# A decoder layer on one core: first x tile on another queue and engine, attention's small products grouped and pinned, the recurrence's diagonal with level 0

## Chip, cores, metric

One core of a Trainium2 chip runs the kernel. The metric is the device time of one execution in microseconds. Engines are named as in the profile: PE (TensorE), PEld (its weight loads), DVE (VectorE), ACT (ScalarE), POOL (GpSimd) and SP (SyncE, which issues most transfers).

## What is computed

One layer on 256 tokens with 2048 features, all in float32:

```
h = RMSNorm(x)
[q_a|k_a|v_a|q_r|f_r|i_r|g_r|gate_a|gate_r] = h @ w_in
A: causal attention, 8 heads of 128, q and k normed per head, partly rotated
R: HGRN2: f = lb + (1-lb) sigmoid(f_r), k = 1-f, q = silu(q_r)
   S_t = diag(f_t) S_{t-1} + k_t i_t^T,  o_t = S_t^T q_t
   o_r = RMSNorm per head (o) * sigmoid(g_r)
y = sigmoid(gate_a + b_a) * (o_a @ w_up_a) + sigmoid(gate_r + b_r) * (o_r @ w_up_r)
x = x + y @ w_out
x = x + relu(RMSNorm(x) @ w_mlp1)^2 @ w_mlp2
```

With 256 tokens there is a single attention block, so the choice of past blocks falls away and attention is plain causal attention.

## The kernel before

Every weight matrix is read in units of 128 x 2048 numbers (1 MB). A unit is loaded by SP into `raw`, ScalarE rounds it to `hi` (float32r), and VectorE makes the rest `lo = raw - hi`. Activations are cut in the same two parts, side by side in tiles called `xcat`, `oac`, `orc` and so on. A product of two matrices is then three streamed products, hi x hi, lo x hi and hi x lo, with 512 columns each, or one of 512 and one of 256 columns where the weights are the stationary side. `cut(u)` (line 170) makes the halves of unit u; `unit()` (line 196) hands out a unit and cuts the one two places ahead. `raw`, `hi` and `lo` have three buffers each. In the stages that stream the weights (`by_tokens`, line 695, and the first loop, line 341) a unit is 24 products, and its second product already wants `lo`.

The units come in this order: 16 for v and i (`pv`), 40 for the projections to q, k, f, g in feature-major form (`project`, groups of two units, `pw`), then for each half of the output columns 16 units of gates (`pg`) and 8 units of the two up-projections (`pr` for the recurrence's output, `pa` for attention's), then w_out and the MLP. TensorE takes the stream's products one after the other; eleven products on zeros (`WARM`, line 231) stand in front.

Beside the stream run generators: `prepare` (line 291, row norms of x, biases, the lower bound lb), `attend` (599), `enter` and `recur` (421, 444) and `recur_out` (572). `step()` (line 207) advances the first two of the list `side` after each group of stream products, by as much work as their yields declare against a budget of 2.8 or 3.6 us. Where one of their small products is issued, it lands in TensorE's order between the stream's: an insertion. The final order on each engine is settled when the program is built, by a scheduler that follows dependencies and its own estimates; `tc.issue_after(x)` keeps an instruction from standing ahead of x.

`attend` makes, for a group of four heads, the scores (`pl`) of the first 128 queries, their softmax, the transposes (`ptr`), then the same for the second 128, then the products with v (`po`). `recur` makes the diagonal blocks of the recurrence (`pd`, line 456), then eight levels, each of which needs q and k multiplied on by the level before. `recur_out` norms the output (`head_rms`, line 550: `pb`, logarithm, exponential on ScalarE), gates it and cuts it into `orc`. `drain()` (line 218) runs all generators to their end ahead of the up-projections.

At the start SP issues the first unit in four pieces with x's tiles in between (`load`, line 146; `load_x`), ScalarE's queue issues the vectors `vt`, and `parts_of_x` (271) cuts x, scaled by the norm's gain, into `xcat`: the high part on ScalarE, the rest on VectorE.

Of the kernel before, what the change touches and what calls it, by code (L numbers as in the profile page):

```python
# [9 lines left out]
F32 = mybir.dt.float32  # L10
# [16 lines left out]
WARM = 11  # L27
# [3 lines left out]
def layer_kernel(ctx: ExitStack, tc: tile.TileContext, xT, vecs, wv, wm, wg, wu, wo, w1, w2, cf, cm, out):  # L31
# [106 lines left out]

    raws = {}
# [6 lines left out]
    def load(u):  # L146
# [3 lines left out]
        for s in pieces(u):  # L150
            if u < 4:
                load_x(u, s)
# [17 lines left out]
    def cut(u):  # L170
# [9 lines left out]
        split[u] = (hi, lo)  # L180
        if u in beside:
# [45 lines left out]
    nc.scalar.dma_start(vt, vecs)  # L227
    warm = pool["g"].tile([P, 512], F32R, tag="g", name="warm")
    nc.vector.memset(warm.bitcast(F32), 0.0)
# [30 lines left out]
    nc.vector.memset(ones_r.bitcast(F32), 1.0)  # L260
    ones = cp.tile([P, P], F32, name="ones")
    nc.vector.memset(ones, 1.0)
    eps_t = cp.tile([P, 1], F32, name="eps_t")
    nc.vector.memset(eps_t, EPS)
    lsc_t = cp.tile([P, 1], F32, name="lsc_t")
    nc.vector.memset(lsc_t, float(-0.5 * np.log(128.0)))
# [22 lines left out]
    lb = cp.tile([P, 2, NH], F32, name="lb")  # L289

    def prepare():
# [28 lines left out]
        lbm = cp.tile([P, NH], F32, name="lbm")  # L320
        lbe = cp.tile([P, 2, NH], F32, name="lbe")
        nc.vector.tensor_max(lbm, lbl[:, 0, :], lbl[:, 1, :])
        for i in range(2):
            nc.vector.tensor_sub(lbe[:, i, :], lbl[:, i, :], lbm)
        nc.scalar.activation(lbe, lbe, AF.Exp)
        nc.vector.tensor_add(lbm, lbe[:, 0, :], lbe[:, 1, :])
        nc.vector.reciprocal(lbm, lbm)
        nc.vector.tensor_mul(lb[:, 0, :], lbe[:, 0, :], lbm)
        nc.vector.tensor_scalar(lb[:, 1, :], lb[:, 0, :], -1.0, 1.0, op0=OP.mult, op1=OP.add)
# [11 lines left out]
    for c in range(4):  # L341
        pst = [bank(f"pv{t}", pm) for t in range(2)]
        for q in range(4):
            hi, lo = unit()
            hi, lo = (x.rearrange("p (k f) -> p k f", k=4) for x in (hi, lo))
            for k in range(4):
                kk = 4 * q + k
                for t in range(2):
                    xh = xcat[:, kk, t * P : (t + 1) * P]
                    xl = xcat[:, kk, T + t * P : T + (t + 1) * P]  # L350
                    nc.tensor.matmul(pst[t], xh, hi[:, k, :], start=(kk == 0), stop=False)  # L351
                    nc.tensor.matmul(pst[t], xh, lo[:, k, :], start=False, stop=False)  # L352
                    nc.tensor.matmul(pst[t], xl, hi[:, k, :], start=False, stop=(kk == KD - 1))  # L353
# [850 lines left out]
```

## Time and profile before

| | |
|---|---|
| time, median of 3 runs | 1388.30 us (1388.20 to 1388.41) |
| the profiled execution: its time, its span | 1388.16 us, 1386.4 us |
| mean granted TensorE clock | 0.999 |
| PE busy | 1380.2 us (100%) |
| PEld, DVE, ACT, POOL busy | 1180.4, 1085.4, 793.6, 82.4 us |
| HBM | 260 GB/s over the span |

The span runs from the first to the last instruction; 1.8 us of the execution lie around it. Busy time of PE is the union of its products with modelled ends, so 100% does not say that each product ran at its best. In the rows further below, times are microseconds from the span's start.

### The profile page before, as it was taken

The numbers are of one execution on the slowest core, as the hardware profiler recorded it, in microseconds if no ns is written. First come the engines' busy times: TensorE is split into PE (matmuls) and PEld (weight loads), VectorE is DVE, ScalarE is ACT, GpSimd is POOL, SyncE is SP. The second block draws the span as 40 slices with busy tenths as digits, with TensorE's granted clock in tenths as the row PEclk, the third lists the DMA queues.
The fourth block names the chain that finished last, engine by engine and source line by source line (L and its number), as shares of the span: only waits on it lengthen the run. The fifth ranks groups of instructions, "written<-read, shape, count | busy, mean of one in ns | idle before, by whom it ended". The sixth has DMA issues, their size and how long they took to land.

```text
span 1386.4 us, 19141 instructions
## 1 busy us (share of the span) xinstructions
PE 1380.2 (100%) x7886; PEld 1180.4 (85%) x7886; DVE 1085.4 (78%) x971; ACT 793.6 (57%) x747; POOL 82.4 (6%) x132
## 2 busy tenths in 40 slices
PE   9999999999999999999999999999999999999998
PEld 7888888888888888888888888888888888888887
DVE  7656789877957776678755979989898888989875
ACT  7444566764457443434445677666666666656652
POOL 0111101001000111111100000000000000000000
PEclk9999999999999999999999999999999999999999
DMA  8898877566765999898966686777868777686772
GB/s 304 312 349 316 304 276 249 202 218 199 258 215 172 333 329 318 294 333 295 324 225 223 223 295 220 260 256 256 288 213 277 239 271 242 241 306 228 278 230 87
DMA packets 108153, 362.35 MB, mean 261 GB/s; under 512 B 8176, under 2 KB 10496, under 8 KB 87840
## 3 DMA queue, kind: packets, MB, share of 16 engines
q1 hardware_dynamic: 88880, 294.99, 61.4%
q0 software_dynamic: 17888, 65.04, 13.0%
q8 instruction: 62, 1.02, 0.3%
q10 hardware_dynamic: 1296, 1.09, 0.3%
q14 instruction: 27, 0.22, 0.0%
HBM read 327.52 MB, written 33.57 MB: 260 GB/s over the span
## 4 chain that ended last, share of the span: by engine, by line
PE 98%; DVE 0%; DMA 0%; ACT 0%; issue 0%; SPq 0%; DVEq 0%
PE pw L368 21%; PE pw L370 11%; PE pw L378 11%; PE pw L381 5%; PE pg L691 4%; PE pg L693 4%; PE pg L692 4%; PE ps L691 3%; PE ps L692 3%; PE ps L693 3%; PE py L691 2%; PE py L692 2%; PE py L693 2%; PE pv L352 2%; PE pv L353 2%; PE pv L351 2%
## 5 line engine op out<-in xcount | busy, mean ns | idle before, releaser
L179 DVE TENSOR_TENSOR lo<-raw,hi 128x2048 fp32r<-128x2048 f32 (+2 forms) x130 | 275.4, 2124 | 133.4 <-ACT hi L178 120.8
L178 ACT ACTIVATE hi<-raw 128x2048 fp32r<-128x2048 f32 (+2 forms) x130 | 231.1, 1782 | 237.4 <-PE pg L693 56.5
L788 DVE TENSOR_TENSOR low<-w,hiw 128x2048 fp32r<-128x2048 f32 x135 | 308.7, 2286 | 66.2 <-ACT hiw L787 63.2
L787 ACT ACTIVATE hiw<-w 128x2048 fp32r<-128x2048 f32 x135 | 258.5, 1915 | 149.3 <-PE pw L368 63.1
L368 PE MATMUL pw<-x2cat,hiw 128*128 128x512 f32 x1024 | 242.8, 389 | 0.0
L368 PEld LDWEIGHTS pw<-x2cat,hiw 128*128 128x128 f32 x1024 | 191.6, 188 | 39.5
L378 PE MATMUL pw<-xcat,hi 128*128 128x512 f32 x640 | 150.2, 391 | 0.0
L378 PEld LDWEIGHTS pw<-xcat,hi 128*128 128x128 f32 x640 | 119.2, 188 | 24.5
L370 PEld LDWEIGHTS pw<-x2cat,low 128*128 128x128 f32 x1024 | 131.3, 191 | 5.0
L370 PE MATMUL pw<-x2cat,low 128*128 128x256 f32 x1024 | 132.8, 283 | 0.0
L691 PE MATMUL pg<-hi,xcat 128*128 128x512 f32 x256 | 100.7, 393 | 0.0
L693 PE MATMUL pg<-hi,xcat 128*128 128x512 f32 x256 | 99.7, 389 | 0.0
L692 PE MATMUL pg<-lo,xcat 128*128 128x512 f32 x256 | 99.7, 389 | 0.0
L788 DVE TENSOR_TENSOR low<-b,hiw 128x2048 fp32r<-128x2048 f32 x35 | 80.2, 2290 | 21.0 <-ACT hiw L787 20.9
L787 ACT ACTIVATE hiw<-b 128x2048 fp32r<-128x2048 f32 x35 | 67.0, 1915 | 30.5 <-PE ps L693 20.3
L381 PEld LDWEIGHTS pw<-xcat,lo 128*128 128x128 f32 x640 | 79.4, 192 | 1.6
L381 PE MATMUL pw<-xcat,lo 128*128 128x256 f32 x640 | 79.9, 283 | 0.0
L368 PE MATMUL pw<-mcat,hi 128*128 128x512 f32 x256 | 61.8, 392 | 0.0
L693 PEld LDWEIGHTS pg<-hi,xcat 128*128 128x128 f32 x256 | 48.1, 188 | 10.1
L691 PEld LDWEIGHTS pg<-hi,xcat 128*128 128x128 f32 x256 | 48.1, 188 | 9.9
L692 PEld LDWEIGHTS pg<-lo,xcat 128*128 128x128 f32 x256 | 48.1, 188 | 9.7
L368 PEld LDWEIGHTS pw<-mcat,hi 128*128 128x128 f32 x256 | 46.9, 188 | 9.0
(266 smaller groups left out, 2234.6 us busy)
## 6 DMA issues: line engine op xcount, KB each, us to landing
w<-w SPq DMA_DIRECT2D x107, 1024.0 KB, 5.6
raw<-wm SPq DMA_DIRECT2D x56, 1024.0 KB, 7.1
wt<-w POOLq DMA_DIRECT2D x56, 512.0 KB, 7.7
t<-wt POOLq DMA_DIRECT2D x56, 512.0 KB, 7.1
w<-t SPq DMA_DIRECT2D x28, 1024.0 KB, 5.1
b<-w SPq DMA_DIRECT2D x21, 1024.0 KB, 6.3
raw<-wg SPq DMA_DIRECT2D x16, 1024.0 KB, 7.1
raw<-wu SPq DMA_DIRECT2D x16, 1024.0 KB, 7.7
```

Source lines behind the costliest of these rows:

```text
L178: nc.scalar.activation(hi[:, s], raw[:, s], AF.Copy)
L179: low = nc.vector.tensor_sub(lo[:, s], raw[:, s], hi[:, s].bitcast(F32))
L351: nc.tensor.matmul(pst[t], xh, hi[:, k, :], start=(kk == 0), stop=False)
L368: nc.tensor.matmul(pst, h, cat, start=(first and i == 0), stop=False)
L370: nc.tensor.matmul(pst[:, T:], l, cat[:, :T], start=False, stop=(last and i == n - 1))
L378: nc.tensor.matmul(pst, h, cat, start=(i == 0), stop=False)
L381: nc.tensor.matmul(pst[:, T:], l, cat[:, :T], start=False, stop=(i == len(parts) - 1))
L691: nc.tensor.matmul(pst, xh, hi[:, k], start=(begin and k == 0), stop=False)
L692: nc.tensor.matmul(pst, xh, lo[:, k], start=False, stop=False)
L693: nc.tensor.matmul(pst, xl, hi[:, k], start=False, stop=(end and k == 3))
L787: nc.scalar.activation(hi, r, AF.Copy)
L788: newest[0] = nc.vector.tensor_sub(lo, r, hi.bitcast(F32))
```

## The change

- The four tiles of x that go with the first unit are loaded by four issues of ScalarE's queue, right behind `vt`, in tiles of 128 x 256. SP's list starts with the four pieces of the first unit.
- The high part of x's first tile is made by VectorE (`tensor_scalar`), the other fifteen by ScalarE as before. In the first unit the three products of the two token halves are issued as hi, hi, lo-of-x, lo-of-x, lo, lo.
- Ten warm-up products in place of eleven. Four small memsets come behind the one that clears the warm-up tile. The lower bound lb is computed after the low half of unit 8.
- `attend` makes the scores of both query halves in one insertion, then one reciprocal and both multiplications, then all transposes, then all products with v. Transposes and value products may not stand ahead of the newest product of the stream in `ws_group`.
- `recur` issues the diagonal and level 0 without a yield in between; the diagonal's products may not stand ahead of `rqp`.
- The up-projection of attention's output comes first, the recurrence's second, and the units of `wu` are loaded in that order.

```diff
-WARM = 11
+WARM = 10
...
-        units += [block(wu, c, at) for c in two for at in (2, 3, 0, 1)]
+        units += [block(wu, c, at) for c in two for at in range(4)]
...
         for s in pieces(u):
-            if u < 4:
+            if 0 < u < 4:
                 load_x(u, s)
...
+    xr.append(g4("xr", (P, 4, T)))
+    for k in range(4):
+        nc.scalar.dma_start(xr[0][:, k, :], xT[0][:, k, :])
     warm = pool["g"].tile([P, 512], F32R, tag="g", name="warm")
...
-            nc.scalar.activation(xcat[:, k, :T], src, AF.Copy, scale=g_in[:, k : k + 1])
+            if k == 0:
+                nc.vector.tensor_scalar(xcat[:, k, :T], src, g_in[:, :1], 1.0, op0=OP.mult, op1=OP.mult)
+            else:
+                nc.scalar.activation(xcat[:, k, :T], src, AF.Copy, scale=g_in[:, k : k + 1])
...
+        with tc.issue_after(lows[8].ins):
+            lower_bound()
...
+                products = [[(p, xh, hi, 0), (p, xh, lo, 1), (p, xl, hi, 2)] for p, xh, xl in tokens]
+                if c + q == 0:
+                    products = [[a[i] for a in products] for i in (0, 2, 1)]
...
+                with tc.issue_after(entered[-1].ins):
+                    nc.tensor.matmul(
+                        pd[32 * b : 32 * b + 32, i * 32 : (i + 1) * 32],
+                        kss[g][:, h, c], qs[g][:, h, c], start=True, stop=True,
+                    )
...
-        yield 0.7
         for lv in range(LEVELS):
...
-            yield 1.5 * (t + 1)
-            nc.vector.reciprocal(sm[:, c], sm[:, c])
-            nc.vector.tensor_mul(l, l, sm[:, c][:, :, None].to_broadcast([P, 4, w]))
-            yield 0.6 * (t + 1) + 0.2
+        yield 4.0
+        nc.vector.reciprocal(sm, sm)
+        for t, l in both:
+            c = slice(4 * t, 4 * t + 4)
+            nc.vector.tensor_mul(l, l, sm[:, c][:, :, None].to_broadcast([P, 4, (t + 1) * P]))
+        yield 5.6
+        for t, l in both:
             for s in range(t + 1):
                 ptr = bank("ptr")
-                for h in range(4):
-                    nc.tensor.transpose(ptr[:, h * P : (h + 1) * P], l[:, h, s * P : (s + 1) * P], ident)
+                with tc.issue_after(stream_end[0].ins):
+                    for h in range(4):
+                        nc.tensor.transpose(ptr[:, h * P : (h + 1) * P], l[:, h, s * P : (s + 1) * P], ident)
...
-            yield 0.1
+        yield 5.6
         for b in range(2):
             po = bank("po")
...
-            for pst in by_tokens(orc, "pr"):
+            for pst in by_tokens(oac, "pa"):
                 pass
...
-            for q, pst in enumerate(by_tokens(oac, "pa")):
+            for q, pst in enumerate(by_tokens(orc, "pr")):
```

The built program's order shows where this leaves the instructions. ScalarE, from the recurrence's last norm to the first units of the up-projections, before (`sq_3843` is the second head group's factor, `orc_3972` and `orc_3975` are the first group's output, `hi_3982` is the first unit of `pr`):

```order
L565 ACT_TABLE_LOAD
L565 ACTIVATE sq_3843<-pb_3931,eps_t 128x512
L565 ACTIVATE sq_3843<-pb_3935,eps_t 128x512
L178 ACTIVATE hi_3942<-raw_3940 128x2048
L568 ACT_TABLE_LOAD
L568 ACTIVATE sq_3843<-sq_3843 128x1024
L410 ACTIVATE orc_3972<-ro_3773 128x2x256
L410 ACTIVATE orc_3975<-ro_3773 128x2x256
L178 ACTIVATE hi_3982<-raw_3980 128x2048
```

The same stretch in the change, from the wider start of the norm on (`hi_3992` is the second unit of `pa`, `hi_4056` the first of `pr`):

```order
L180 ACTIVATE hi_3992<-raw_3990 128x2048
L589 ACT_TABLE_LOAD
L589 ACTIVATE sq_3907<-pb_3977,eps_t 128x512
L589 ACTIVATE sq_3907<-pb_3981,eps_t 128x512
L592 ACT_TABLE_LOAD
L592 ACTIVATE sq_3907<-sq_3907 128x1024
...
L747 ACT_TABLE_LOAD
L747 ACTIVATE gate_4033<-gate_4033 128x512
L592 ACT_TABLE_LOAD
L592 ACTIVATE sq_3945<-sq_3945 128x1024
L432 ACTIVATE orc_4038<-ro_3873 128x2x256
L432 ACTIVATE orc_4041<-ro_3873 128x2x256
L180 ACTIVATE hi_4056<-raw_4054 128x2048
```

Both norms' factors, with a gate's sigmoid between, now stand in one run behind `hi_3992`, and the next unit's hi comes only after them.

VectorE in that stretch, before:

```order
L411 TENSOR_TENSOR orc_3972<-ro_3773,orc_3972 128x2x256
L411 TENSOR_TENSOR orc_3975<-ro_3773,orc_3975 128x2x256
L577 SCALAR_TENSOR_TENSOR ro_3790<-ro_3790,vt,sq_3843 128x1024
L179 TENSOR_TENSOR lo_3983<-raw_3980,hi_3982 128x2048
L578 TENSOR_TENSOR ro_3790<-ro_3790,sgr_2730 128x1024
L179 TENSOR_TENSOR lo_4019<-raw_4016,hi_4018 128x2048
```

and in the change:

```order
L602 TENSOR_TENSOR ro_3873<-ro_3873,sgr_2456 128x1024
L601 SCALAR_TENSOR_TENSOR ro_3890<-ro_3890,vt,sq_3945 128x1024
L433 TENSOR_TENSOR orc_4038<-ro_3873,orc_4038 128x2x256
L433 TENSOR_TENSOR orc_4041<-ro_3873,orc_4041 128x2x256
L602 TENSOR_TENSOR ro_3890<-ro_3890,sgr_2678 128x1024
L181 TENSOR_TENSOR lo_4057<-raw_4054,hi_4056 128x2048
L433 TENSOR_TENSOR orc_4046<-ro_3890,orc_4046 128x2x256
```

`lo_4057`, the low half of `pr`'s first unit, moved behind the scaling, the cutting and the gating of the recurrence's output.

TensorE where `pr` begins in the change (`pa` ends above it, with the third of its products):

```order
L724 MATMUL pa_306_4053<-hi_3992,oac_2901 128x512
L722 MATMUL pr_307_4118<-hi_4056,orc_4038 128x512
L722 MATMUL pr_308_4119<-hi_4056,orc_4038 128x512
L723 MATMUL pr_307_4118<-lo_4057,orc_4038 128x512
L724 MATMUL pr_307_4118<-hi_4056,orc_4038 128x512
```

and before:

```order
L693 MATMUL pg_297_3898<-hi_3942,xcat 128x512
L691 MATMUL pr_305_4053<-hi_3982,orc_3972 128x512
L692 MATMUL pr_305_4053<-lo_3983,orc_3972 128x512
L693 MATMUL pr_305_4053<-hi_3982,orc_3972 128x512
L691 MATMUL pr_305_4053<-hi_3982,orc_3972 128x512
```

In the change 48 products lie between the last `pb` and `pr`, before 72; and the first two products of `pr` are now both of the hi half.

## Rows read from the trace of the kernel before

**Rows 1.** The page, part 4: the chain that ended last, by engine.

```profile
PE 98%; DVE 0%; DMA 0%; ACT 0%; issue 0%; SPq 0%; DVEq 0%
```

**Rows 2.** Timeline, TensorE, start: start us, us, line, tile, count [idle <-releaser].

```profile
1.46 4.76 PE L232 MATMUL pwarm<-warm 128*128 128x512 f32 x11 [1.46 <-DVE warm L229]
...
6.37 0.19 PEld L351 LDWEIGHTS pv<-hi,xcat 128*128 128x128 f32 x1 [0.57 <-ACT xcat L274]
...
10.04 0.39 PE L351 MATMUL pv<-hi,xcat 128*128 128x512 f32 x1
```

**Rows 3.** Timeline, TensorE, 420 to 428 us: the two last norms' products.

```profile
420.41 0.39 PE L563 MATMUL pb<-sqh,ones_r 128*128 128x512 f32 x1
...
421.33 0.39 PE L691 MATMUL pg<-hi,xcat 128*128 128x512 f32 x1
...
426.78 0.39 PE L563 MATMUL pb<-sqh,ones_r 128*128 128x512 f32 x1
...
427.71 0.39 PE L691 MATMUL pg<-hi,xcat 128*128 128x512 f32 x1
```

**Rows 4.** Timeline, TensorE: value products of both groups; the stream behind an insertion.

```profile
259.08 0.39 PE L653 MATMUL po<-pt,v 128*128 128x128 f32 x2
...
261.68 1.63 PE L378 MATMUL pw<-xcat,hi 128*128 128x512 f32 x6
...
310.22 0.39 PE L653 MATMUL po<-pt,v 128*128 128x128 f32 x2
...
313.11 7.54 PE L378 MATMUL pw<-xcat,hi 128*128 128x512 f32 x32
...
342.54 0.50 PE L691 MATMUL pg<-hi,xcat 128*128 128x512 f32 x1
342.87 0.39 PE L692 MATMUL pg<-lo,xcat 128*128 128x512 f32 x1
```

**Rows 5.** Timeline, ScalarE, 420 to 440 us: norm of the recurrence's output.

```profile
420.61 1.92 ACT L178 ACTIVATE hi<-raw 128x2048 fp32r<-128x2048 f32 x1 [3.53 <-PE pg L693]
422.54 1.28 ACT L565 ACT_TABLE_LOAD   x1
423.84 1.27 ACT L565 ACTIVATE sq<-pb,eps_t 128x512 f32<-128x512 f32 x2
...
426.42 0.63 ACT L716 ACTIVATE gate<-gate 128x512 f32<-128x512 f32 x1
...
428.36 1.06 ACT L568 ACTIVATE sq<-sq 128x1024 f32<-128x1024 f32 x1
...
438.04 1.14 ACT L410 ACTIVATE orc<-ro 128x512 fp32r<-128x512 f32 x2
```

**Rows 6.** Timeline, VectorE, 439 to 447 us.

```profile
439.13 1.28 DVE L411 TENSOR_TENSOR orc<-ro,orc 128x512 fp32r<-128x512 f32 x2
440.34 1.28 DVE L577 SCALAR_TENSOR_TENSOR ro<-ro,vt,sq 128x1024 f32<-128x1024 f32 x1
...
443.74 1.22 DVE L578 TENSOR_TENSOR ro<-ro,sgr 128x1024 f32<-128x1024 f32 x1
444.87 2.29 DVE L179 TENSOR_TENSOR lo<-raw,hi 128x2048 fp32r<-128x2048 f32 x1
```

**Rows 7.** Timeline, ScalarE, first 16 us.

```profile
5.80 0.91 ACT L274 ACTIVATE xcat<-xr,vt 128x256 fp32r<-128x256 f32 x2
7.36 0.63 ACT L178 ACTIVATE hi<-raw 128x512 fp32r<-128x512 f32 x1 [0.65 <-DMA raw<-wv]
...
15.36 1.06 ACT L178 ACTIVATE hi<-raw 128x1024 fp32r<-128x1024 f32 x1 [0.38 <-DMA raw<-wv]
```

**Rows 8.** Timeline, VectorE, the fourth unit's first low half.

```profile
22.22 1.22 DVE L179 TENSOR_TENSOR lo<-raw,hi 128x1024 fp32r<-128x1024 f32 x1
```

**Rows 9.** Timeline, VectorE, attention's first group: mask addition, larger multiplication.

```profile
223.63 0.68 DVE L624 TENSOR_TENSOR l<-pl,consts 128x512 f32<-128x512 f32 x1
...
247.27 1.22 DVE L638 TENSOR_TENSOR l<-l,sm 128x1024 f32<-128x1024 f32 x1
```

More of the change, by code (lines that the diff above doesn't have):

```diff
@@ L137, in layer_kernel @@
     split = {}
+    lows = {}
     raws = {}
@@ L180, in cut @@
         split[u] = (hi, lo)
+        lows[u] = low
         if u in beside:
@@ L289, in layer_kernel, with lower_bound @@
     lb = cp.tile([P, 2, NH], F32, name="lb")
+    def lower_bound():
+        lbm = cp.tile([P, NH], F32, name="lbm")
+        lbe = cp.tile([P, 2, NH], F32, name="lbe")
+        nc.vector.tensor_max(lbm, lbl[:, 0, :], lbl[:, 1, :])
+        for i in range(2):
+            nc.vector.tensor_sub(lbe[:, i, :], lbl[:, i, :], lbm)
+        nc.scalar.activation(lbe, lbe, AF.Exp)
+        nc.vector.tensor_add(lbm, lbe[:, 0, :], lbe[:, 1, :])
+        nc.vector.reciprocal(lbm, lbm)
+        nc.vector.tensor_mul(lb[:, 0, :], lbe[:, 0, :], lbm)
+        nc.vector.tensor_scalar(lb[:, 1, :], lb[:, 0, :], -1.0, 1.0, op0=OP.mult, op1=OP.add)
     def prepare():
@@ L319, in prepare @@
         nc.gpsimd.dma_start(bias_rows, flat)
[L320 to L329, printed above, removed]
+        with tc.issue_after(lows[8].ins):
+            lower_bound()
         yield 1.0
@@ L347, in layer_kernel @@
                 kk = 4 * q + k
[L348 to L353, printed above, removed]
+                tokens = [
+                    (pst[t], xcat[:, kk, t * P : (t + 1) * P], xcat[:, kk, T + t * P : T + (t + 1) * P]) for t in range(2)
+                ]
+                products = [[(p, xh, hi, 0), (p, xh, lo, 1), (p, xl, hi, 2)] for p, xh, xl in tokens]
+                if c + q == 0:
+                    products = [[a[i] for a in products] for i in (0, 2, 1)]
+                for p, x, w, i in sum(products, []):
+                    nc.tensor.matmul(
+                        p, x, w[:, k, :], start=(kk == 0 and i == 0), stop=(kk == KD - 1 and i == 2)
+                    )
             if c == 0 and q == 3:
@@ L380, in ws_group @@
             for i, (h, l, cat) in enumerate(parts):
-                nc.tensor.matmul(pst[:, T:], l, cat[:, :T], start=False, stop=(i == len(parts) - 1))
+                stream_end[0] = nc.tensor.matmul(
+                    pst[:, T:], l, cat[:, :T], start=False, stop=(i == len(parts) - 1)
+                )
         return ps
+    stream_end = [None]
     def unit_parts(hi, lo, cats, off=0):
@@ L612, in attend @@
         l1 = g4("l1", (P, 4, T))
-        for t, l in ((0, l0), (1, l1)):
+        both = ((0, l0), (1, l1))
+        for t, l in both:
             w = (t + 1) * P
@@ L646, in attend @@
                 pt.append(d)
[L647 removed]
+        yield 5.6
         for b in range(2):
             po = bank("po")
[L650 to L655 removed]
+            with tc.issue_after(stream_end[0].ins):
+                for j in range(2):
+                    h = 2 * b + j
+                    hc = slice((4 * g + h) * P, (4 * g + h + 1) * P)
+                    at, to = po[:, j * T : j * T + P], po[:, j * T + P : (j + 1) * T]
+                    nc.tensor.matmul(at, vv[0][:, hc], pt[0][:, h, :], start=True, stop=True)
+                    nc.tensor.matmul(to, vv[0][:, hc], pt[1][:, h, :], start=True, stop=False)
+                    nc.tensor.matmul(to, vv[1][:, hc], pt[2][:, h, :], start=False, stop=True)
             oc = g4("oac", (P, 2, 512), F32R)
```

31 lines of the change are left out of this document (13 added, 18 removed).

## Prediction

> **What bounds the kernel now.** I read the page first: the chain of waits that ended last lies on TensorE for 98% of the span [rows 1]. Nothing that VectorE, ScalarE or a queue saves counts unless TensorE waits for it, and whatever makes TensorE wait is added to the time in full. So I look for three things only: TensorE's waits that the change removes, TensorE's own cycles that it saves, and new waits.
>
> The next view is the timeline of the first 10 us, engine by engine. Eleven warm-up products on zeros start at 1.46, and the first real product at 6.37 after 0.57 us idle behind ScalarE's xcat [rows 2]. The thirteenth starts at 10.04. A 512-column product in the stream takes 0.227 us (24 products from 421.33 to the next insertion at 426.78 [rows 3]), so an unbroken stream that reaches 10.04 there would have begun at 10.04 - 12 x 0.227 = 7.32. I call that the stream's virtual start: what moves it, and nothing else at this end, moves the time.
>
> After that the timeline shows TensorE running through attention, the recurrence and the gates with small products inserted between the stream's. The reader is to see there what an insertion costs beyond its columns [rows 4], and at 420 to 446 us how long ScalarE and VectorE take from the recurrence's last norm to the next unit's halves [rows 5, 6].
>
> **The change, part by part.**
>
> *Start.* Removed: one warm-up product, one small Exp on ScalarE, seven tiny VectorE operations, two issues on SP ahead of the weights. Added: four issues on ScalarE's queue, and x's first tile is rounded on VectorE beside ScalarE's first hi, instead of after hi and the Exp. The first product then needs neither [rows 7]. The tenth warm-up product leaves TensorE free about 0.4 us earlier, at some 5.8. If it starts then and nothing waits later, the gain is 7.32 - 5.83 = 1.49. But the stream is fed just in time: the first low half of the fourth unit ends at 22.22 + 1.22 = 23.44 [rows 8], and it is the 74th product's (three units of 24 products, then one hi). 23.44 - 73 x 0.227 = 6.87: with that feed the gain stops at 7.32 - 6.87 = 0.45, wherever the first product starts. ScalarE feeds that part without a break from 15.36 on, and there it had waited 0.38 us for a transfer [rows 7]. The relief on ScalarE ahead of it (the Exp and one xcat, 0.45) only lengthens that wait; the feed moves with the transfers. SP's two issues fewer can bring them forward, the queue shared with x can hold them back. Bad end: x's first tile lands as late as the second raw piece did, 7.36 [rows 7], the product starts at about 7.9 and runs through: a loss of 0.6. I take a gain of 0.6, near the 0.45 that the feed's row gives. The Trainium skill, "DMA: Bandwidth & Descriptors", section Rules for kernel authors, says that spreading DMAs over issuing engines saves only the sequencer's issue time; by it the feed stays where it is, the gain is 0.45 and the forecast 0.15 higher; no row of before has two data queues at the start.
>
> *Attention in fewer insertions.* The same products stay, so columns are not saved. What goes: in the second group the value products (po) take 313.11 - 310.22 = 2.89 us, in the first 261.68 - 259.08 = 2.60 [rows 4]; the 0.29 is a wait for the last transposed tile, copied only just before, which now has a stretch of stream to land in. And two insertions fewer (one here, one for the diagonal): the stream's first product after one takes 342.87 - 342.54 = 0.33 instead of 0.227, so 0.1 each. Together 0.5 saved. The bounds: 0.2 if a new short wait takes the place of the old one; 1.0 if splits such as that of the key norm save as much again. The cover that must hold: scores of both halves now go in one insertion, and the transposes follow 64 stream products later (32 wide, 32 half-wide, 11 us). In between lie, one behind the other, three mask additions of 0.65, two maxima, a low half (2.29 [rows 6]), four exponentials on ScalarE and the two multiplications, 1.22 the larger [rows 9]. With 0.5 for an exponential, which is near an xcat, and a maximum priced like the operation of its size in these rows, that is 1.95 + 1.9 + 2.3 + 2.0 + 1.9 = 10.1 us, an estimate. Some 1 us of slack is left in the first group, more in the second, where eight more products lie between.
>
> *Recurrence.* Diagonal and level 0 go together, 128 products in one insertion, and pinned behind rqp. VectorE has 48 stream products (10.9 us) after the value products to make rqp; two low halves, two oac parts, rks and rqp fit in. I cost it at nothing beyond the 0.1 above.
>
> *The recurrence now ends later, the up-projection comes sooner.* This is the term that decides. Attention's second group takes the places where the recurrence stood, so the last norm (pb) now goes in directly ahead of the up-projection, two units ahead of the first product that needs the recurrence; before, it was three. The swap of pa and pr is what leaves these two. I follow the chain by durations of the same operations in before, with zero at the start of the first pb (420.41 [rows 3]).
>
> ScalarE: hi of the unit being fed ends at 422.53, that is 2.12 [rows 5]. Then, in the order now built: table load, logarithm pair, load, exponential, load, gate, load, logarithm pair, load, gate, load, exponential. Six loads at 1.30 from start to next start (422.54 to 423.84), two logarithm pairs of 1.28, two gates of 0.65, two exponentials of 1.07 [rows 5]: 7.80 + 2.56 + 1.30 + 2.14 = 13.80. The second head's factor is there at 15.92. The two orc copies (1.1) and then hi of the recurrence's unit (1.92) end at 18.9.
>
> VectorE stands at the second ro, waiting for that factor, and the order puts the low half of the recurrence's unit behind it: scaling 1.19, the orc pair 1.21, the gating 1.13, and the low half itself 2.29 [rows 6]. 15.95 + 1.19 + 1.21 + 1.13 + 2.29 = 21.77.
>
> TensorE: the second pb is over at 427.71, 7.30 [rows 3], and 48 products later, at 7.30 + 10.90 = 18.20, it reaches pr. Its first two products take the hi half, the third the low half; that one would start at 18.65 and starts at about 21.8. **A wait of 3.1 us**, all of it on TensorE. In the old order the low half of pr's first unit stands ahead of the gating, a further unit of gate products lies between, and no wait is in the rows. Behind the wait the next unit's low half would be ready about 0.5 us before it is needed, so one wait and not two.
>
> The Trainium skill, "ScalarE: Activation LUTs", section What ACT_TABLE_LOAD costs, puts each switch at about 2.66 us with a drain. The rows show the next activation 0.02 us after a load's end. By the page the six loads would take 8.2 us more and the time would be 1398.4.
>
> *The rest.* The order of wu's blocks, lower_bound's place and the swapped multiplications move work that TensorE does not wait for in these rows; nothing.
>
> **Sum.** -0.6 - 0.5 + 3.1 = +2.0 us. The profiled execution took 1388.16; the median of the runs is 1388.30, 0.14 above, so one serves for the other: 1388.16 + 2.0 = **1390.2 us**, 0.14% slower. About 0.2% (2.8 us) is what a measurement of this kernel can tell from no change, so this falls in the same class.
>
> **Rivals.**
>
> 1. *The recurrence's unit is ready in time* (some of ScalarE's chain overlaps more than the order says, or TensorE comes later). For it: in before the same operations never held TensorE up. Against it: the chain is 12 rows in one engine's order with known durations, and it would have to shrink by 3 of 16 us. Time: 1388.16 - 1.1 = 1387.1; with the start's best end 1386.2. This is the rival on the other side; it decides if the low half is ready by 18.65 on the clock above.
> 2. *The start goes wrong*: x's first tile, behind the vectors on ScalarE's queue, lands with the second raw piece. Loss 0.6 instead of a gain of 0.6: 1391.4. It decides at a landing later than 6.8 or so.
> 3. *The transposes wait for the softmax*: 1 us of slack, and one low half (2.29 [rows 6]) falling ahead of the multiplications uses it up: 1.3 more in a group, 1391.5; in both 1392.8.
> 4. *The pinning does not hold*: the second group's transposes already stand in two insertions, two products apart. It keeps 0.1 to 0.2 of the 0.5: 1390.4, inside the forecast.
> 5. *Table loads with a drain*, as the page has it: 1398.4. The rows speak against it.
>
> **How the numbers follow.** Forecast (with rival 4) 0.66, rival 1 0.14, rival 2 0.09, rival 3 0.10, rival 5 0.01. The forecast's own range is 1389.0 to 1391.2, from the start's gain of 1.2 to 0 and the insertions' 1.0 to 0.2, with 0.3 either way on the wait. Rival 1 spreads over 1386.2 to 1387.8, so a range from 1387.0 leaves out about half of it; 1391.6 at the top leaves out the worse part of rivals 2 and 3. Faster by over 0.2% needs 1385.5, below the best ends of start and insertions together (1388.16 - 1.5 - 1.0): 0.03. Slower by over 0.2% needs 1391.1: rivals 2, 3 and 5 in good part: 0.15. Within: 0.82.
>
> **What would show it.** In the profile after: a wait of TensorE behind VectorE's low half at the first pr, 2.5 to 3.5 us, the second largest after the warm-up's; pv starting at 5.8 to 6.2 and the 144th product 0.3 to 1 us earlier than before; no gap ahead of ptr or pd; the value products of both groups at 2.6 us. I am wrong if pr starts without a wait, or if ptr has one.

## The result: 11.6 us slower, and the profile after

The kernel before took 1388.25 us (median of 6 runs, 1387.63 to 1389.02), the changed kernel 1399.84 us (6 runs, 1398.12 to 1401.56). The ratio is 1.0084 with a 95% interval of 1.0071 to 1.0097. The forecast was 1390.2 us and its range ended at 1391.6. The sign was right, the size was not.

The profiled execution took 1399.84 us with a span of 1398.1, 11.7 more than before. The chain of the page is still on TensorE, as in [rows 1], now with 97%:

```profile
PE 97%; ACT 1%; DMA 1%; DVE 1%; issue 0%; ACTq 0%; DVEq 0%
```

The waits of TensorE in the changed kernel (line waited for: us in total, times, longest us):

```profile
PE pd L500 <- issue: 4.5, 1, 4.5
PE pr L723 <- DVE lo L181: 2.3, 1, 2.3
PE pwarm L238 <- DVE warm L235: 1.5, 1, 1.5
PE pv L369 <- DVE xcat L282: 0.9, 1, 0.9
PE pr L722 <- ACT hi L180: 0.5, 1, 0.5
```

To see what each is worth I cut both timelines at the same products of TensorE and compared the stretches:

| stretch on TensorE | before | after | difference |
|---|---|---|---|
| to the start of the last pv product | 95.38 | 96.47 | +1.09 |
| to the first product of the up-projections (444.03; 450.95) | 348.65 | 354.48 | +5.83 |
| to the last of their 384 products (620.60; 632.46) | 176.57 | 181.51 | +4.94 |
| to the end of the span | 765.8 | 765.6 | -0.2 |

**Second stretch.** The timeline of TensorE where the diagonal (L481) and level 0 (L500) now stand together:

```profile
347.34 1.29 PE L481 MATMUL pd<-rq,rks 128*32 128x32 f32 x126
...
348.48 0.40 PE L500 MATMUL pd<-rqp,rks 128*32 128x16 f32 x27
353.41 1.10 PE L500 MATMUL pd<-rqp,rks 128*32 128x16 f32 x99 [4.53 <-issue]
354.44 0.80 PE L722 MATMUL pg<-hi,xcat 128*128 128x512 f32 x1
355.03 0.63 PE L723 MATMUL pg<-lo,xcat 128*128 128x512 f32 x1
355.46 0.63 PE L724 MATMUL pg<-hi,xcat 128*128 128x512 f32 x1
```

After 27 and 2 products of level 0 TensorE stands for 4.53 us, and the row names no releaser, only "issue": it waited for nothing that the profile shows. Between the stream's products this insertion takes 354.44 - 347.02 - 0.227 = 7.20 us, where in the kernel before the two took 1.34 and 1.29. That is +4.57. The two rows of the kernel before, without a gap:

```profile
324.41 1.32 PE L456 MATMUL pd<-rq,rks 128*32 128x32 f32 x128
336.97 1.27 PE L476 MATMUL pd<-rqp,rks 128*32 128x16 f32 x128
```

Behind the gap the stream's products start 0.43 us apart instead of 0.227 until 357.6: another 1.6. What is left of the stretch, attention with it, is a gain of 0.3.

**Third stretch.** TensorE at the first product of pr:

```profile
461.60 0.39 PE L724 MATMUL pa<-hi,oac 128*128 128x512 f32 x1
462.46 0.73 PE L722 MATMUL pr<-hi,orc 128*128 128x512 f32 x2 [0.47 <-ACT hi L180]
465.48 0.50 PE L723 MATMUL pr<-lo,orc 128*128 128x512 f32 x1 [2.28 <-DVE lo L181]
...
467.03 0.63 PE L723 MATMUL pr<-lo,orc 128*128 128x512 f32 x1
467.46 0.63 PE L724 MATMUL pr<-hi,orc 128*128 128x512 f32 x1
```

The wait that the prediction worked out is there: 0.63 us for the hi half and 2.45 for the low half beyond a stream product, 3.08 together. From 467 to 470 us the products are again 0.43 apart, 1.6 us more. The windows of the changed kernel show what that is (columns: stretch; its length and the busy time of PE, PEld, DVE, ACT, POOL; granted clock; DMA share; GB/s):

```profile
355.00:357.00 2.00, 2.00 (x6) 1.58 (x5) 2.00 (x5) 0.00 (x0) 0.00 (x0) 0.50 0.64 244
468.00:470.00 2.00, 2.00 (x6) 1.54 (x5) 2.00 (x2) 0.00 (x0) 1.26 (x2) 0.50 1.05 412
```

The granted clock is 0.50 there, the lower of its two levels (1.2 instead of 2.4 GHz), each time behind a stretch in which TensorE stood; in the kernel before it is 1.00 in all these windows.

**First stretch.** The first product of pv starts at 7.00 instead of 6.37 [rows 2], behind x's first tile, and the weights' fourth piece comes late as well (10.77, the second row of ScalarE; the last row is the kernel before, where the third and fourth piece are rounded without a wait):

```profile
7.00 1.17 PE L369 MATMUL pv<-hi,xcat 128*128 128x512 f32 x4 [0.91 <-DVE xcat L282]
6.50 0.35 DVE L282 TENSOR_SCALAR xcat<-xr,vt 128x256 fp32r<-128x256 f32 x1 [4.80 <-DMA xr<-xT]
7.59 0.51 ACT L284 ACTIVATE xcat<-xr,vt 128x256 fp32r<-128x256 f32 x1 [1.70 <-DMA raw<-wv]
10.77 0.63 ACT L180 ACTIVATE hi<-raw 128x512 fp32r<-128x512 f32 x1 [0.83 <-DMA raw<-wv]
...
8.82 1.21 ACT L178 ACTIVATE hi<-raw 128x512 fp32r<-128x512 f32 x2
```

**Attention.** There is no wait at ptr in either group. The value products of the second group go from 333.64 to 336.24, 2.60 us instead of 2.89 [rows 4]; the transposes there still stand in two insertions, of 4 and of 8.

```profile
333.64 0.39 PE L684 MATMUL po<-pt,v 128*128 128x128 f32 x2
...
336.24 0.47 PE L722 MATMUL pg<-hi,xcat 128*128 128x512 f32 x1
```

### The profile page after: what moved, and what is told of

Read it like the earlier page. It is cut to its first block, busy times and chain, and to the rows that moved or that the text cites. A ratio compares the mean times of both kernels' runs of the same rounds, so it can differ in the third digit from the quotient of the medians.

```text
span 1398.1 us, 19159 instructions
## 1 busy us (share of the span) xinstructions
PE 1384.1 (99%) x7885; PEld 1181.9 (85%) x7885; DVE 1086.7 (78%) x970; ACT 790.3 (57%) x744; POOL 81.3 (6%) x132
## 3 DMA queue, kind: packets, MB, share of 16 engines
q8 instruction: 62, 1.02, 0.3%
## 4 chain that ended last, share of the span: by engine, by line
PE 97%; ACT 1%; DMA 1%; DVE 1%; issue 0%; ACTq 0%; DVEq 0%
PE pw L386 21%; PE pw L388 11%; PE pw L396 10%; PE pv L369 6%; PE pw L399 5%; PE pg L722 4%; PE pg L724 4%; PE pg L723 4%; PE ps L722 3%; PE ps L723 3%; PE ps L724 3%; PE py L722 2%; PE py L723 2%; PE py L724 2%; PE pe L723 2%; PE pe L724 2%
## 5 line engine op out<-in xcount | busy, mean ns | idle before, releaser
L369 PE MATMUL pv<-hi,xcat 128*128 128x512 f32 x256 | 78.8, 391 | 0.9 <-DVE xcat L282 0.9
L369 PEld LDWEIGHTS pv<-hi,xcat 128*128 128x128 f32 x256 | 47.8, 188 | 12.1 <-issue 1.6
```

Source lines behind the costliest of these rows:

```text
L369: nc.tensor.matmul(p, x, w[:, k, :], start=(kk == 0 and i == 0), stop=(kk == KD - 1 and i == 2))
```

## The experiments

Times are medians, beside the kernel before on the same chip (its medians there: 1388.2 to 1388.5).

### The gap of 4.5 us: two bursts of tiny products

The page of the changed kernel lists a DMA queue for instructions, and `PE` and `PEld` with 7885 instructions each, 15,770 / 62 = 254 for each of its packets (16 KB each, by 1.02 MB / 62):

```profile
q8 instruction: 62, 1.02, 0.3%
```

So theory S: TensorE's instructions arrive in packets, and 128 tiny products in a row (256 rows of products and as many weight loads) use them up faster than the next packet comes. In **e1_apart** the two bursts are apart again:

```diff
             pd.rearrange("p (i t) -> p i t", i=16),
         )
+        yield 0.7
         for lv in range(LEVELS):
```

> The changed kernel with the diagonal and level 0 apart again (the yield between them back, the pinning kept). Theory S (TensorE runs out of instructions when 128 tiny products follow each other: the gap of 4.53 us at 348.9 has no releaser, and the only 16 KB instruction packet near it starts at 351.04): the gap goes and so does the stretch at half clock behind it, 4.5 + 1.6 = 6.1 us, so 1399.8 - 6.1 = 1393.7 us (1392.8 to 1394.6); the two insertions cost about 1.3 each and the clock is full from 340 to 360 us. Rival D (TensorE waits there for an operand, rqp or the memory behind near, because of the pinning): the pinning is kept, so the gap stays, in front of the diagonal or of level 0, and the time is 1398 to 1400. Between them, if the gap goes but the clock falls anyway: 1395.3.

Measured: 1394.13 us (1393.69 to 1398.12), ratio 1.0050 [1.0038, 1.0063], 5.7 less than the changed kernel. The insertions cost 1.34 and 1.32, the clock is full there. The gap is gone from the burst, so D falls. But a smaller one came one unit later, in the middle of the stream, where nothing tiny runs. That the time fits is partly luck: the second stretch is 351.19, only 3.3 less than in the changed kernel. Another 2.0 come from the third (179.51), where TensorE now waits at pr for the recurrence's output itself and the clock stays full (the last row):

```profile
356.04 0.39 PE L724 MATMUL pg<-lo,xcat 128*128 128x512 f32 x1
359.07 0.39 PE L725 MATMUL pg<-hi,xcat 128*128 128x512 f32 x1 [2.64 <-issue]
...
PE pr L723 <- ACT orc L432: 2.0, 2, 1.2
```

In **e2_twice** the kernel before multiplies the diagonal twice, with operands long ready:

```diff
-        for i, (g, h, t) in enumerate(cols):
+        for i, (g, h, t) in 2 * list(enumerate(cols)):
```

> The kernel before, with the recurrence's diagonal multiplied twice in a row: the same 64 products, with the same operands and into the same bank, follow themselves, so that 128 tiny products stand together and nothing new has to be waited for. Theory S: a gap of about 4.5 us without a releaser inside the diagonal, a stretch at half clock behind it (1.6), and 1.1 for the products themselves: 1388.3 + 7.2 = 1395.5 us (1393.5 to 1396.5). Rival D (an operand was late): only the products are added, 1389.4 us (1389.0 to 1389.8), and no gap.

Measured: 1391.30 us (1391.09 to 1392.64), ratio 1.0023 [1.0013, 1.0032]. That is +2.8 where S said 7.2 and D 1.1. Gaps without a releaser there are, though no operand is new; but they are short: one in the burst, one in the stream behind it, and a third in a later level of the recurrence, at 369.19 us. The mechanism stands, its price is not a constant:

```profile
324.17 1.40 PE L456 MATMUL pd<-rq,rks 128*32 128x32 f32 x141
325.96 1.21 PE L456 MATMUL pd<-rq,rks 128*32 128x32 f32 x115 [0.39 <-issue]
327.10 3.24 PE L378 MATMUL pw<-xcat,hi 128*128 128x512 f32 x13
331.33 4.49 PE L378 MATMUL pw<-xcat,hi 128*128 128x512 f32 x19 [0.99 <-issue]
...
PE pd L476 <- issue: 0.7, 1, 0.7
```

What the gaps share shows when TensorE's instructions (products, weight loads and its sequencer's records) are counted up to each of them: 4033 in the changed kernel and in every experiment that keeps the merged burst; 4289 = 4033 + 256 in e1_apart; 3777 = 4033 - 256, 4033 again, and 5569 = 4033 + 6 x 256 in e2_twice. Every wait of TensorE that the trace puts down to "issue" lies a multiple of 256 instructions from the others, at the boundary of a packet, and work goes on 1.2 to 1.6 us after the packet has landed that brings the next instruction. What differs is when the packet starts. In the changed kernel no TensorE packet (q8) starts from 328 to 351 us, and one does at 351.04 (the DMA view of two stretches; columns: packets, MB, share of 16 engines):

```profile
q1 hardware_dynamic: 2091, 4.15, 52.2%
q0 software_dynamic: 144, 0.52, 5.6%
q14 instruction: 1, 0.01, 0.1%
...
q8 instruction: 1, 0.02, 5.9%
```

A unit of the gates' weights was issued at 346.27 and landed at 351.57: the packet came when that transfer was nearly over. To compare packets, take as a mark the instruction that stands 321 ahead of the first one that a packet brings; no packet of the thirteen profiles starts before it. In the kernel before three packets from 338 to 347 us start 1.2 to 1.3 us after it (the other queues' share of the DMA engines from mark to start is 0.00, 0.32 and 0.00). In the changed kernel this one starts 4.7 us after it, which is also the median where that share is over 0.6 (51 packets, 1.9 to 10.9). Theory S2 is thus that the packet stands behind the weights. In **e12_load_held** the loads of units 62 to 64 are held back, by a memset that follows level 1:

```diff
         raws[u] = wp.tile([P, UW], F32, tag="raw", name=f"raw{u}")
+        if u in (62, 63, 64):
+            with tc.issue_after(level_done[1].ins):
+                nc.vector.memset(raws[u][:, :1], 0.0)
...
-                nc.vector.copy_predicated(
+                level_done[lv] = nc.vector.copy_predicated(
```

> The changed kernel with the loads of three units (62, 63, 64: the last two of the first gate's weights and the next) held back until level 1 of the recurrence is copied; they are needed 27 us and more after they were issued at 346.3, so they may wait. In every profile so far TensorE stopped exactly at a boundary of its 16 KB instruction blocks, and the packet with the next block started only when a unit's transfer was nearly over (351.04, with the unit landing at 351.57); where no transfer ran, a packet came 1.2 to 2.6 us after the middle of the block before. Theory S2 (the packet stands behind the weights' packets): with no transfer under way the packet starts by 349.0 instead of 351.0, the gap is 1.0 to 2.5 us instead of 4.5, and the clock may stay: 1396.6 us (1394.8 to 1397.6). Rival S1 (the packet comes late because of the burst, whatever the other queues do): the gap stays at 4.3 to 4.7 us, 1399.8 us.

Measured: 1398.50 us (1396.63 to 1398.85), ratio 1.0067 [1.0054, 1.0079]. The gap is at the same instruction, 4033, and less than half as long, and nothing but the packet and the end of one store runs beside it:

```profile
348.86 0.40 PE L504 MATMUL pd<-rqp,rks 128*32 128x16 f32 x27
351.35 0.85 PE L504 MATMUL pd<-rqp,rks 128*32 128x16 f32 x65 [2.09 <-issue]
```
```profile
q0 software_dynamic: 57, 0.17, 5.3%
q8 instruction: 1, 0.02, 1.0%
```

S2 holds for a part of the gap: the packet started at 348.73, and 2.4 of the 4.53 us went with the weights. The other 2.1 stay, though nothing else was under way: the packet still starts 2.0 us after its mark, and the burst has used up its instructions before it lands. The time, outside the expected range, fell by 1.3 and not by 3.2: the clock still fell behind the gap, the held units cost a wait of 0.5 us behind a low half near 380 us, and a later level's insertion at 386 us takes 2.01 instead of 1.32.

### The wait at pr: what is it for?

In **e3_pr_later** the third unit of the up-projections is attention's, not the recurrence's:

```diff
-        units += [block(wu, c, at) for c in two for at in range(4)]
+        units += [block(wu, c, at) for half in (0, 2) for c in two for at in (half, half + 1)]
...
-        for i, c in enumerate(two):
-            ga, gr = gates[i], gates[2 + i]
+        for ga in gates[:2]:
             for pst in by_tokens(oac, "pa"):
                 pass
             for t in range(2):
                 nc.vector.tensor_mul(ga[:, t, :], pst[t], ga[:, t, :])
+        for i, c in enumerate(two):
+            ga, gr = gates[i], gates[2 + i]
             for q, pst in enumerate(by_tokens(orc, "pr")):
```

> The changed kernel with both column blocks of attention's up-projection ahead of the recurrence's (pa, pa, pr, pr instead of pa, pr, pa, pr). Theory Q (the wait is for the low half of the third unit, which stands behind the recurrence's scaling and gating in VectorE's order, whatever that unit belongs to): the wait of 2.3 us stays at the third unit, which is now pa's, and the half clock behind it too; 1399.8 us (1398.8 to 1400.8). Rival R (pr waits because it needs the recurrence's output, which is late): pr now comes 48 products or 10.9 us later, the wait and the half clock go, 3.1 + 1.7: 1395.0 us (1394.2 to 1395.8).

Measured: 1399.71 us (1399.27 to 1400.87), ratio 1.0085 [1.0071, 1.0099]. TensorE's waits (the same columns as above) name pa, which needs nothing of the recurrence:

```profile
PE pa L723 <- DVE lo L181: 2.3, 1, 2.3
PE pa L722 <- ACT hi L180: 0.5, 1, 0.5
```

R falls. The half clock did not come as expected: behind this wait the clock stays at 1.00, and the third stretch is 1.6 shorter than in the changed kernel; the second is 1.0 longer, with the clock at 0.50 for longer behind the gap. That the time fits is luck. In **e7_recurrence_late**, on top of this edit, the second norm starts one unit later and `drain()` stands behind pa, so that halves come first in both engines' order:

```diff
         while ro[g] is None:
             yield 0.0
+        if g == 1:
+            yield 0.0
...
-        drain()
         for ga in gates[:2]:
...
+        drain()
         for i, c in enumerate(two):
```

> The changed kernel with pa, pa, pr, pr as in e3_pr_later, and with the end of the recurrence's norm written one unit later and not forced ahead of the up-projections, so that in ScalarE's and VectorE's order the halves of the third and fourth unit stand ahead of the second norm's factor and its scaling. Theory Q (the wait at the third unit is for halves that stand behind the recurrence's output in both engines' order): wait and half clock go, 3.1 + 1.7, although the recurrence now ends later: 1395.0 us (1394.2 to 1396.0), and the gap of 4.5 us at 349 stays. Rival R (TensorE waits for the recurrence's result or for ScalarE as such): a wait of 2 us or more stays at one of the units from the third to the sixth, 1398 or more.

Measured: 1395.77 us (1394.18 to 1396.15), ratio 1.0052 [1.0039, 1.0064]: 4.1 less, with the recurrence ending later (the last of `orc` at 470.3 instead of 466.6). The wait is gone, the gap stays; these are its longest waits:

```profile
PE pd L500 <- issue: 4.2, 1, 4.2
PE pwarm L238 <- DVE warm L235: 1.5, 1, 1.5
PE pv L369 <- DVE xcat L282: 0.9, 1, 0.9
```

### The start

**e4_old_start** puts the old start into the changed kernel, the old order of the first unit's products too:

```diff
-WARM = 10
+WARM = 11
...
-            if 0 < u < 4:
+            if u < 4:
...
-    xr.append(g4("xr", (P, 4, T)))
-    for k in range(4):
-        nc.scalar.dma_start(xr[0][:, k, :], xT[0][:, k, :])
...
-            if k == 0:
-                nc.vector.tensor_scalar(xcat[:, k, :T], src, g_in[:, :1], 1.0, op0=OP.mult, op1=OP.mult)
-            else:
-                nc.scalar.activation(xcat[:, k, :T], src, AF.Copy, scale=g_in[:, k : k + 1])
+            nc.scalar.activation(xcat[:, k, :T], src, AF.Copy, scale=g_in[:, k : k + 1])
...
-                if c + q == 0:
-                    products = [[a[i] for a in products] for i in (0, 2, 1)]
```

> The changed kernel with the start of the kernel before: x's first tiles by SP between the pieces of the weights, all sixteen high parts of x on ScalarE, eleven warm-up products, the old order of the first unit's products; the rest as changed. Theory B (the start costs time, because the four small transfers take four of the eight that may be under way, and SP's fourth piece of the weights is issued at 5.4 instead of 3.1 us): the 144th product of the stream starts at about 39.8 instead of 41.0, and the time is 1399.8 - 1.2 = 1398.6 us (1397.8 to 1399.3). Rival (the start gains the 0.6 of the prediction, and the rest of the change costs more than it seems): 1400.4 us.

Measured: 1400.03 us (1399.51 to 1401.36), no gain. The profile says more than the time: the 144th product starts at 39.51 instead of 41.03, but at 63.77 TensorE waits behind a low half, and the last pv product starts at 96.12, only 0.35 earlier. Then the clock stays at 0.50 longer behind the gap (10 products at 0.43 us, where the changed kernel's profile has 6; the second stretch is 1.45 longer) and does not fall behind pr's wait (the third is 1.6 shorter). In **e10_start_and_bound** the lower bound goes back as well:

```diff
-        with tc.issue_after(lows[8].ins):
-            lower_bound()
+        lower_bound()
```

> As e4_old_start (the old start in the changed kernel), and the lower bound computed where it was, in the first 9 us, instead of behind unit 8. In e4_old_start the 144th product came 1.5 us earlier than in the changed kernel, but the stream lost 1.0 us at 62.5 us behind a low half that stands behind the lower bound's operations. Theory L (the moved lower bound causes that wait, and hides what the start costs): no wait at 62.5, last product of the first stage at about 95.4 instead of 96.5, 1398.7 us (1398.0 to 1399.3). Rival (the wait comes from when the weights land beside the sums of w2, not from the lower bound): it stays, 1399.6 to 1400.2.

Measured: 1399.92 us (1398.42 to 1401.40). The last pv product starts at 95.76, 0.7 earlier than in the changed kernel; the wait at 63 us is still there with 0.22 instead of 0.84: the lower bound explains part of it at most. A new gap of 0.7 us stands at instruction 5313 = 4033 + 5 x 256, 388.8 us. Runs of kernels with the merged burst scatter by 1.5 to 3.5 us, so one of 1 us can't be read from their times. **e14_start_alone** is the kernel before with the diff of e4_old_start reversed, and nothing else of the change but the memsets behind the warm-up tile's.

> The kernel before with the change's start alone: x's first tiles in four transfers on ScalarE's queue, the first high part of x on VectorE, ten warm-up products, the new order in the first unit. Theory X (x's first tile shares the memory with SP's second piece of the weights and lands at 6.4 instead of 5.7, and the feed of the first units comes later): first product at 6.6 to 7.0, last product of the first stage at 96.0 to 96.5 instead of 95.4, 1389.1 us (1388.6 to 1389.7). Rival P (the prediction's term: the start gains 0.6): last product of the first stage at 94.8, 1387.7 us. Rival N (what is lost at the start is made up by the wait near 63 us that e4_old_start showed): 1388.3 us.

Measured: 1389.00 us (1388.74 to 1392.51), ratio 1.0006 [0.9998, 1.0015]; the last pv product starts at 96.40, 1.02 later than before. The times alone do not tell the two kernels apart (the interval holds 1); the shift is read from the profile. **e6_two_x** loads x's tiles in two transfers instead of four:

```diff
-    for k in range(4):
-        nc.scalar.dma_start(xr[0][:, k, :], xT[0][:, k, :])
+    for k in (0, 2):
+        nc.scalar.dma_start(xr[0][:, k : k + 2, :], xT[0][:, k : k + 2, :])
```

> The changed kernel with x's first four tiles in two transfers of 256 KB on ScalarE's queue instead of four of 128 KB; all else as changed. Theory B (eight transfers may be under way; four small ones of x fill the places, so SP's fourth piece of the weights is issued at 5.42 instead of 3.07 us and the feed of the first units is late): SP issues that piece at 3.1 us again, it lands at 8.5 to 9.5 instead of 10.74, and the 144th product of the stream starts at 39.7 to 40.4 instead of 41.0; of that about 0.7 to 1.0 reaches the end of the first stage, 1399.0 us (1398.3 to 1399.6). Rival W (it is the late first product, 7.00 instead of 6.37, with x on the second queue, that costs): the first product stays at 7.0 or later, the 144th at 40.8 to 41.3, and the time at 1399.8.

Measured: 1399.44 us (1398.51 to 1400.03). SP issues the fourth piece at 2.11 instead of 5.42, it lands at 9.00 instead of 10.74, and yet the 144th product starts at 41.25: early weights are not enough. Its first seven products start at least 0.43 us apart without a wait between them, the pace of the half clock, and the trace's record of the full clock begins at 10.4 us, in the kernel before at 5.75:

```profile
7.20 2.05 PE L369 MATMUL pv<-hi,xcat 128*128 128x512 f32 x4 [1.11 <-ACT xcat L284]
```

The virtual start (the n-th product's start less n x 0.2266 us) shows where each start loses:

| product | before | e14_start_alone | after | e6_two_x |
|---|---|---|---|---|
| 0 | 6.37 | 6.54 | 7.00 | 7.20 |
| 18 | 7.42 | 7.07 | 7.46 | 8.84 |
| 36 | 7.42 | 8.06 | 8.12 | 8.84 |
| 60 | 7.43 | 8.23 | 8.33 | 8.84 |
| 143 | 7.43 | 8.55 | 8.63 | 8.84 |

In e14_start_alone the first unit does run 0.35 ahead of before. Then the second, third and fourth unit each come late (ScalarE's first hi of the second unit starts at 12.14, in the kernel before at 10.84). With two transfers the loss stands ahead of product 18, in those products at half clock, and behind it the stream comes later (8.84) than the changed kernel's feed would have let it (8.63). So e6_two_x decides neither B nor W, and what makes the feed late stays open.

The other profiles hold the loss and not the gain. Product 143 has a virtual start of 8.14 to 8.99 in the six with the change's start (the changed kernel, e1, e3, e7, e12, e14) and of 7.10 to 7.43 in the six with the old one (the kernel before, e2, e4, e10, e11, e13). At product 18 e7 and e12 have 8.66 and 8.58, with seven and eight products at half clock as in e6; the other four have 7.05 to 7.46, the old start 6.59 to 7.42, with two products at half clock at most. The warm-up product taken out may cost the clock there; no run parts it from the rest of the start.

### All three losses out

**e11_all_undone** has the edits of e1, e7 and e10 together.

> All three losses taken out of the changed kernel: start and lower bound as before (e10), diagonal and level 0 apart (e1), the recurrence's end behind the first units of the up-projections (e7). What stays of the change is attention's grouping and the recurrence's place beside the gates. By the terms: 1388.3 - 0.2 (attention), and the gap of 2.6 us that e1_apart showed at the second boundary of instruction blocks if the recurrence's bursts fall there again: 1390.7 us (1388.0 to 1391.2). If instead the losses overlap and each repair uncovers another, 1392 or more.

Measured: 1391.40 us (1390.01 to 1393.77), ratio 1.0025 [1.0015, 1.0036]. That is 0.2 above the expected range. The stretches of the table above, in the profile of its run of 1390.01, are 95.18, 349.18 and 177.51; the second holds a gap of 1.5 us at instruction 4289, and 0.9 of the third are products of a norm (pb) that stand in the second elsewhere. In **e13_undone_held** the three loads are held back as in e12.

> As e11_all_undone (start, lower bound, diagonal and the recurrence's end undone), with the same three loads held back until level 1 is copied. Theory S2: the gap of 1.9 us that e11_all_undone shows at the second block boundary goes or falls under 0.5, and so do the slower runs of that kernel (its runs reach from 1390.0 to 1393.8): 1388.3 us (1387.6 to 1389.3), about the kernel before. Rival S1: as e11_all_undone, 1391.4 us (1390.4 to 1392.4). If the held units come too late for the gates, a wait behind a low half near 375 us or later, 1390 or more.

Measured: 1391.72 us (1389.13 to 1395.23, 11 runs), ratio 1.0022 [1.0012, 1.0032]. The gap at 4289 is gone, but the held loads now run beside later levels, and in the profiled run a packet starts 9.5 us after its mark, with a gap at 5569 = 4033 + 6 x 256. The held units also come too late for the gates, as the expectation allowed, with a wait of 1.23 us behind a low half at 375.77:

```profile
392.00 0.39 PE L721 MATMUL pg<-lo,xcat 128*128 128x512 f32 x1
395.35 0.39 PE L722 MATMUL pg<-hi,xcat 128*128 128x512 f32 x1 [2.96 <-issue]
...
PE pg L721 <- DVE lo L184: 1.2, 1, 1.2
```

Five of the eleven runs took 1389.1 to 1389.8, the others 1391.7 to 1395.2. S2 is borne out for the place, and moving the transfers only moved the collision. The median of none of these kernels lies below that of the kernel before.

## Why the prediction was wrong, step by step

- **Recurrence, "I cost it at nothing": the step that failed, +6.2 instead of 0.** The prediction gave a reason why rqp would be ready in time, and none why 128 tiny products in a row should cost TensorE no more than 64 and 64. No row of the kernel before has 128 of them in a row, so the operation should have been bounded from above. The gap is 4.5 us of missing instructions and 1.6 of half clock; e12_load_held parts the 4.5 into 2.4 for the weights' transfer ahead of the packet and 2.1 for the burst itself. The move of the recurrence beside the gates matters as much as the merging: from 347 to 353 us there the DMA share is 0.54, while from 335 to 350 us of the kernel before, where three of its bursts stand, it is 0.22 on the mean. Each by itself costs the second stretch about the same, 2.5 us for the new place without merging (e1_apart) and 2.6 beyond the products for a double burst in the old place (e2_twice: 3.74 - 1.1); together it is 5.8.
- **The wait at pr: right to 0.1 us, but its consequence was left out.** Every stage of the chain came as worked out: with zero at the first pb (443.65) the factor is ready at 459.56 - 443.65 = 15.9 and the low half at 21.8. The rows of ScalarE and VectorE:

```profile
457.21 1.28 ACT L592 ACT_TABLE_LOAD   x1
458.50 1.06 ACT L592 ACTIVATE sq<-sq 128x1024 f32<-128x1024 f32 x1
460.51 3.70 ACT L180 ACTIVATE hi<-raw 128x2048 fp32r<-128x2048 f32 x2
```
```profile
459.60 1.29 DVE L601 SCALAR_TENSOR_TENSOR ro<-ro,vt,sq 128x1024 f32<-128x1024 f32 x1 [5.76 <-ACT sq L592]
...
462.00 1.22 DVE L602 TENSOR_TENSOR ro<-ro,sgr 128x1024 f32<-128x1024 f32 x1
463.14 2.28 DVE L181 TENSOR_TENSOR lo<-raw,hi 128x2048 fp32r<-128x2048 f32 x1
```

  e3 shows that the wait is one for an engine's order and not for the recurrence's result, as the prediction had it ("the order puts the low half behind it"). What it did not price is TensorE's clock after standing: 1.6 us, and that in three of the six profiles that have this wait. In e1_apart's order it was the recurrence's output itself that came last (2.0 us).
- **Start: wrong sign, +1.0 instead of -0.6.** The bad end in the text was a late first tile of x. That was the smaller part (6.39 instead of 5.72, below the 6.8 from which rival 2 was to decide). The step that failed is "the feed moves with the transfers", followed by a gain: the feed moved, backwards, in units two to four. The first product started at 7.00 and not at 5.8 to 6.2, and the virtual start of the kernel before is 7.42 from product 18 on, not 7.32. The warm-up product taken out was counted as a gain alone. By the Trainium skill, "DMA: Bandwidth & Descriptors", section Rules for kernel authors, spreading saves issue time alone; e14_start_alone shows not even that much left at the end of the stage.
- **Attention: -0.3 of the -0.5.** The rows show the mechanism for the value products (0.29); that nothing else was gained or lost is only the remainder of the stretch, no run has the grouping alone. Rival 4 came true (4 and 8 transposes), rival 3 did not.
- **Rival 1** (no wait) is refuted by the rows, **rival 5** too: a table load takes 1.28 us and the next activation starts 0.01 later.
- **The range** was made from the terms' own bounds (all their ends at once would give 1388.8 to 1391.4, a little wider than written). A term costed at nothing brought no bound into it, and that term was the largest.

The sum as measured: 1.1 + 4.6 + 1.6 - 0.3 + 3.1 + 1.6 = 11.7, the difference of the spans. The -0.3 is a remainder, and 0.2 more in the third stretch and 0.2 less behind it are in no term.

## What to carry to other kernels

An insertion of tiny products has a second price beside its columns: it uses up instructions that come by DMA, and where weights stream, the next packet stands behind them. Quiet DMA queues halved the gap here and did not remove it (4.53 to 2.09), so keep bursts apart, and far from transfers; and look in the trace for gaps with no releaser that lie multiples of 256 instructions apart. A wait of some microseconds on TensorE is to be priced with the half clock that may follow. And where a stage is fed just in time, follow the feed past its first unit before you count a gain at its start.

## What the runs showed of the hardware

- TensorE's instructions come in packets of 16 KB, 256 of them: the gaps without a releaser stand multiples of 256 instructions apart. Each begins 449 instructions past 256 times the packets that have landed (193 where the next packet has landed already and work has not gone on yet). In none of the thirteen profiles does a packet start while more than 298 landed instructions lie ahead. The Trainium skill, "Runtime: NRT & Kernel Launch", section Instruction fetch mechanics, has the 16 KB blocks of 256 instructions and a DMA queue of their own; the trace agrees. Of the memory it says two things: two blocks, which these 298 and the 256 of the next packet fit roughly, and 2048 instructions for TensorE, which no trace here bears out. It calls the cost of a block's boundary mostly hidden; so it is in the kernel before, where none of 62 packets leaves a gap, but in the changed kernel one costs 4.53 us.
- The granted clock fell to 0.50 behind every gap of 4.1 us or more (six profiles), behind the one of 2.96 (e13) and the one of 2.09 (e12), but not behind the one of 2.64 (e1), and behind the wait of 2.28 at the third unit in three of six. How long it stayed there differed too: 10 products stand at 0.43 us behind the gap in e4, 6 in the changed kernel.

**Open.** The trace does not show when a packet is asked for, so how long it stands behind weights is known only by its start. What makes the clock fall behind one wait and not behind an equal one was not tried. The small wait near 63 us is not fully explained: 0.84 us in e4, 0.22 with the lower bound back in e10, none with the same start and bound in e11, and 0.56 in e6 with the new start. Attention's grouping has no run of its own.
